# Compressing keys and values as one chain, with the two first layers side by side in TensorE's columns

## The chip, the cores and the metric

The kernel runs on one core of a Trainium2 chip. The metric is the time on the device in microseconds (us), the median of several executions. The engines are TensorE (PE; PEld is its weight load), VectorE (DVE), ScalarE (ACT) and GpSimd (POOL); SyncE (SP) issues the DMA transfers. Each engine works through its own list of instructions in order, and waits at an instruction until what it needs is there.

## The reference

One layer on 512 tokens of width 1024, in fp32. A norm and one projection (`w_in`) feed two mixers side by side: an attention (NSA) over compressed, selected and windowed keys, and a recurrence over the tokens (RWKV7). Their outputs go through `w_out`, and a feed-forward part (1024 to 4096 to 1024) follows. The change touches the compression: of 512 tokens of keys, and the same of values, 31 overlapping blocks of 32 tokens are formed in each of two heads, and each block of 32 x 64 numbers goes through two layers:

```python
def compress_blocks(kv, pos, w1, w2):
    idx = np.arange(n_cmp)[:, None] * CMP_STRIDE + np.arange(CMP_BLOCK)[None, :]
    blocks = kv[:, idx] + pos[None, None, :, None, :]
    flat = blocks.transpose(0, 1, 3, 2, 4).reshape(B, n_cmp, NSA_KV_HEADS, CMP_BLOCK * HEAD_DIM)
    return jax.nn.gelu(flat @ w1) @ w2          # 2048 -> 128 -> 64

kc = rmsnorm(compress_blocks(kc, ck_pos, ck_w1, ck_w2), kc_g)
vc = compress_blocks(vc, cv_pos, cv_w1, cv_w2)
```

## The kernel before

**Order of the work.** The layer is written as generators (streams), each of which yields the cost of what it has issued and how long to wait before it goes on. `merge` (L129) keeps a clock of these costs and always takes the ready stream of the highest priority: the input projections of RWKV (`rw_in`, `rw_v`) and NSA (`nsa_in`), four token tiles of RWKV preparation (`rw_prep`), inverse (`rw_inv`), values (`rw_vals`) and scan (`rw_chain`), and the attention (`attns`). `run_more` runs the streams that appear later: `compress_both`, `keys` and `queries`. From the program so ordered a scheduler makes the list of each engine. A change in one stream's costs or tiles thus moves its neighbours.

**Buffers.** Tiles in SBUF come from named places with a few buffers each. Where all are taken, the next user waits until the oldest has been read for the last time:

```python
PLACES = {
    'wr': (2144, 2), 'wh': (2144, 3), 'wl': (2144, 3), ...
    'kt': (2048, 8), 'vh': (2048, 4), 'qq': (2048, 7), 'tb': (2048, 1), 'cs': (1024, 4),
}
```

Bytes per partition and number of buffers: `wr` holds `wraw`, the weights as they come from memory, in two buffers. In PSUM `ps`, `pi`, `pq` and `pz` have one bank each, `pa` and `pb` two.

**Projections.** The weights come in pieces (L428): a DMA into `wraw`, a rounded copy `whi` on ACT (L311), the rest `wlo` on DVE (L312), and three products per tile on PE (L332 to 334: hi with hi, lo with hi, hi with lo). The blocks of NSA are `cmp` (columns for the compression), `kv0`, `kv1` (tiles `128x268` on PE, `128x536` for the casts), `q0` and `q1` (`128x256`), four pieces each, and 24 matmuls per piece in `tok_cols` (L836).

**Compression.** `compress` runs for keys (`kind` 0) and then for values (`kind` 1). Its steps: blocks plus positions on POOL (`XP`, 31 blocks of two heads, 62 columns); the first layer `ph` on PE, 16 matmuls with 62 columns of weights and 128 moving columns; gelu on ACT and DVE (`t1`, in the profile `t`, and `gl`); a transpose `pgl`; its copy `gt`; the second layer `pc_`; its copy `cm`. For keys a norm (`cms`, `s`, `rs_yc`), the gain (`cd`), a transpose (`pkt`) and the copy `KCT` follow; for values the copies into `VCM` on POOL. `ROW` names the two halves of the 128 partitions.

**RWKV names.** `pb` (L556) starts DVE's work on a token tile: `kkn` and `mk` (L561, L562), `AR`, `ba`, `BK` (L566, L568; on POOL `k` and another `BK`) and `rkp` (L622). `pg` (L586) multiplies `AR` and `BK`. The inverse goes to and fro between PE and DVE: `pz` and `pd` (L681), `Tn` (L694, then transposed at L671), and at its end `pz<-Tn,QU` (L702). `pv` (L614) and `pbn` (L627) are products whose outputs alternate between the two halves of the partitions.

Of the kernel before, what the change touches and what calls it, by code (L numbers as in the profile page):

```python
# [12 lines left out]
AF = mybir.ActivationFunctionType  # L13
ALU = mybir.AluOpType
AX = mybir.AxisListType


T = 512
# [96 lines left out]
def layer(ctx: ExitStack, tc: tile.TileContext, A, cst, out):  # L115
    nc = tc.nc
    PSUM = bass.MemoryType.PSUM
    V, S, G, PE = nc.vector, nc.scalar, nc.gpsimd, nc.tensor

    def bc(ap, shape):  # L120
        return ap.to_broadcast(shape)
# [5 lines left out]
    done = {}  # L127
# [34 lines left out]
    def bank(tag, n):  # L162
        return lambda shape, name, dt=F32: psA.tile(shape, dt, name=name, tag=tag, bufs=n)

    ps, pi_, pq_, pz_ = bank("ps", 1), bank("pi", 1), bank("pq", 1), bank("pz", 1)
# [10 lines left out]
    def at(place, shape, name, dt=F32):  # L176
        size, n = PLACES[place]
        assert int(np.prod(shape[1:])) * 4 <= size
        return up.tile(shape, dt, name=name, tag=place, bufs=n)
# [10 lines left out]
    def small(n, name):  # L190
        return sm.tile([128, n], F32, name=name, tag=name, bufs=1 if n == 32 else 2)
# [12 lines left out]
    ident = identr.bitcast(F32)  # L204
# [13 lines left out]
    for q in FQ:  # L218
# [9 lines left out]
        else:  # L228
            h = int(q[1])
# [57 lines left out]
    def vec(key, j=0, n=1):  # L287
        return VEC[:, VO[key] + j:VO[key] + j + n]
# [10 lines left out]
    def rsqrt(v, n, key, p=128):  # L299

        y = small(n, "rs_y" + key)[0:p]
        G.tensor_tensor(y, v, bc(MH[0:p], [p, n]), op=ALU.pow)
        return y
# [219 lines left out]
    ROW = (slice(0, 64), slice(64, 128))  # L523
# [295 lines left out]
    GK = cp.tile([128, 3, 64], F32, name="GK")  # L819
    GB = cp.tile([128, 24], F32, name="GB")  # L820
    GT = cp.tile([128, NT, 24], F32, name="GT")
    KCT = cp.tile([128, 2, 32], F32, name="KCT")
    VCM = cp.tile([128, 2, 4, 64], F32, name="VCM")
# [23 lines left out]
        for i in range(NT):  # L847
            use(i, pas[i][:, 0:n])

    def compress(kind, ckv):  # L850

        w1 = [at('kt', [128, 4, 128], "cw1") for _ in range(4)]
        w1v = A[('cmp_k_w1', 'cmp_v_w1')[kind]][0].rearrange("(a p) h -> p a h", p=128)
        for a_ in range(4):
            nc.sync.dma_start(w1[a_], w1v[:, 4 * a_:4 * a_ + 4])
        w2 = at('cs', [128, 64], "cw2")
        nc.sync.dma_start(w2, A[('cmp_k_w2', 'cmp_v_w2')[kind]][0])
        XP = []
        for a in range(2):
            pos = vec('pk' if kind == 0 else 'pv', 8 * a, 8)  # L860
            xp = at('qq', [128, 8, 2, 31], "XP")
            for kv in range(2):
                x2 = ckv[kv][:, 16 * a:T]
                src = bass.AP(tensor=x2.tensor, offset=x2.offset, ap=[x2.ap[0], [2, 8], [16, 31]])
                G.tensor_tensor(xp[:, :, kv, :], src, bc(pos.unsqueeze(2), [128, 8, 31]), op=ALU.add)
            XP.append(xp)
        done['xp', kind] = 1
        yield 0.0, 4.0
        ph = pz_([62, 128], "ph")
        for a_ in range(16):  # L870
            PE.matmul(ph, XP[a_ // 8][:, a_ % 8].rearrange("p a b -> p (a b)"), w1[a_ // 4][:, a_ % 4, :],
                      start=a_ == 0, stop=a_ == 15)
        t1 = at('cs', [62, 128], "t1")
        gl = at('cs', [62, 128], "gl")
        S.activation(t1, ph, AF.Square)
        V.tensor_scalar(t1, t1, 0.044715, 1.0, op0=ALU.mult, op1=ALU.add)
        V.tensor_tensor(t1, t1, ph, op=ALU.mult)
        S.activation(t1, t1, AF.Tanh, scale=math.sqrt(2.0 / math.pi))
        V.scalar_tensor_tensor(gl, t1, 1.0, ph, op0=ALU.add, op1=ALU.mult)
        yield 3.4, 3.0  # L880
        pgl = pz_([128, 2, 31], "pgl")
        PE.transpose(pgl.rearrange("p k n -> p (k n)"), gl, ident[0:62, 0:62])
        gt = at('cs', [128, 2, 32], "gt")
        G.memset(gt[:, :, 31:32], 0.0)
        S.copy(gt[:, :, 0:31], pgl)
        yield 0.2, 1.0
        pc_ = pz_([32, 2, 64], "pc_")
        for kv in range(2):
            PE.matmul(pc_[:, kv, :], gt[:, kv, :], w2, start=True, stop=True)
        cm = at('cs', [32, 2, 64], "cm")  # L890
        S.activation(cm, pc_, AF.Copy, scale=0.5)
        yield 0.5, 5.0
        if kind == 0:
            sq = at('cs', [32, 2, 64], "cms")
            S.activation(sq, cm, AF.Square)
            s2 = small(2, "s2")
            V.tensor_reduce(s2[0:32], sq, axis=AX.X, op=ALU.add)
            V.tensor_scalar(s2[0:32], s2[0:32], 1.0 / 64, 1e-6, op0=ALU.mult, op1=ALU.add)
            r2 = rsqrt(s2[0:32], 2, 'c', p=32)
            V.tensor_tensor(cm, cm, bc(r2.unsqueeze(2), [32, 2, 64]), op=ALU.mult)  # L900
            cd = at('cs', [32, 2, 2, 64], "cd")
            for h in range(2):
                V.tensor_tensor(cd[:, :, h, :], cm, bc(GK[0:32, None, 2, :], [32, 2, 64]), op=ALU.mult)
            pkt = pz_([128, 2, 32], "pkt")
            for kv in range(2):
                PE.transpose(pkt[:, kv, :], cd[:, kv].rearrange("p a b -> p (a b)"), ident[0:32, 0:32])
            S.copy(KCT, pkt)
        else:
            G.memset(VCM, 0.0)
            for h in range(4):  # L910
                G.tensor_copy(VCM[32 * h:32 * h + 32, :, h, :], cm)
        done['cmp', kind] = 1

    def compress_both(ckv):
        for kind in range(2):
            yield from compress(kind, ckv[kind])

    def keys(b, kb):

# [55 lines left out]
    def nsa_in():  # L975
# [10 lines left out]
        yield from feat_cols(512, cmp_in)  # L986
        done['in', 'cmp'] = 1
        more.append((5, compress_both(ckv)))
        kb = [at('qq', [128, NT, 2, 64], "kb") for _ in range(2)]
        for j in range(NT):  # L990
# [276 lines left out]
    w1v = A['w_ff1'][0].rearrange("(k p) n -> p k n", p=128)  # L1267
# [165 lines left out]
```

## Time and profile before

| | |
|---|---|
| median of 3 runs | 785.31 us (785.08 to 786.59) |
| profiled execution | 783.81 us, span 781.9 us |
| mean granted clock of TensorE | 0.987 |
| busy: PE, DVE, ACT, POOL | 759.8, 511.8, 395.6, 175.2 us |
| share of the chain that ended last: PE, DVE, ACT, DMA | 84%, 7%, 4%, 3% |

The span runs from the first to the last instruction of the profiled execution. Busy time counts the instructions of an engine, not its waits. [...] The chain that ended last is followed back from the last instruction, at each step to what released it. The projections, compression and RWKV tiles up to the attention lie between about 100 and 250 us; the feed-forward part begins behind 440 us.

### The profile page before, as it was taken

How to read it: one execution, taken by the hardware profiler on the slowest of the kernel's cores; microseconds unless marked ns; L12 is line 12 of the kernel's file. 1: busy time of each engine (PE TensorE's matmuls, PEld its weight loads, DVE VectorE, ACT ScalarE, POOL GpSimd, SP SyncE). 2: the span in 40 equal slices, each digit the busy share in tenths (PEclk: the TensorE clock that was granted, in tenths of full speed). 3: DMA queues.
4: the chain of work that ended last, by engine and by line, in shares of the span. 5: the costliest groups of instructions: out<-in, count | busy, mean ns of one | idle time of the engine just before them, and what ended most of it. 6: DMA issues, size and time to landing. Idle time of an engine off the chain costs nothing.

```text
span 781.9 us, 18278 instructions
## 1 busy us (share of the span) xinstructions
PE 759.8 (97%) x7357; PEld 657.5 (84%) x7357; DVE 511.8 (65%) x1157; ACT 395.6 (51%) x928; POOL 175.2 (22%) x176
## 2 busy tenths in 40 slices
PE   7999999999989999999999899999999999999998
PEld 5888888889879877887788899998888999978886
DVE  6444385585586789898755888973334989853333
ACT  7343433345444867888544655673332456653330
POOL 5002032240332353434400152300001323100000
PEclk9999999999985999999999999999999999999999
DMA  7741331111000000120343053233323433133212
GB/s 235 206 133 42 94 84 44 44 29 31 15 16 1 29 3 2 30 57 9 114 149 95 17 146 108 69 104 110 96 92 103 118 102 106 62 122 95 95 54 108
DMA packets 67338, 62.00 MB, mean 79 GB/s; under 512 B 6013, under 2 KB 53299, under 8 KB 67254
## 3 DMA queue, kind: packets, MB, share of 16 engines
q1 hardware_dynamic: 67254, 60.83, 25.9%
q8 instruction: 58, 0.95, 0.5%
q14 instruction: 26, 0.21, 0.1%
HBM read 58.72 MB, written 2.10 MB: 78 GB/s over the span
## 4 chain that ended last, share of the span: by engine, by line
PE 84%; DVE 7%; ACT 4%; DMA 3%; issue 1%; SPq 1%; POOL 0%; DVEq 0%; ACTq 0%; POOLq 0%
PE pa L332 8%; PE pa L333 8%; PE pa L334 8%; PE po L332 7%; PE po L333 7%; PE po L334 7%; PE pw L333 5%; PE pw L334 5%; PE pw L332 5%; PE pg L586 2%; PE sc L1075 2%; DMA wraw<-in_w_out_dram 1%; PE py L757 1%; PE pT L1111 1%; PE pz L681 1%
## 5 line engine op out<-in xcount | busy, mean ns | idle before, releaser
L311 ACT CAST whi<-wraw 128x512 fp32r<-128x512 f32 (+1 forms) x128 | 78.7, 622 | 133.4 <-PE po L333 29.1
L312 DVE TENSOR_TENSOR wlo<-wraw,whi 128x512 fp32r<-128x512 f32 (+1 forms) x120 | 86.7, 725 | 86.1 <-ACT whi L311 80.9
L332 PE MATMUL po<-whi 128*128 128x512 f32 x256 | 100.7, 394 | 1.2 <-DVE cc L1361 1.2
L333 PE MATMUL po<-wlo,whi 128*128 128x512 f32 x256 | 101.0, 395 | 0.0
L334 PE MATMUL po<-whi,wlo 128*128 128x512 f32 x256 | 100.7, 393 | 0.0
L333 PE MATMUL pw<-TT,whi 128*128 128x256 f32 x224 | 63.2, 282 | 0.0
L334 PE MATMUL pw<-TT,wlo 128*128 128x256 f32 x224 | 63.0, 281 | 0.0
L332 PE MATMUL pw<-TT,whi 128*128 128x256 f32 x224 | 62.5, 279 | 0.0
L332 PEld LDWEIGHTS po<-whi 128*128 128x128 f32 x256 | 48.0, 188 | 13.0 <-ACT whi L311 1.6
L334 PEld LDWEIGHTS po<-whi,wlo 128*128 128x128 f32 x256 | 48.1, 188 | 11.4
L333 PEld LDWEIGHTS po<-wlo,whi 128*128 128x128 f32 x256 | 48.0, 188 | 11.0
L332 PE MATMUL pa<-XH,whi 128*128 128x512 f32 (+1 forms) x144 | 53.0, 372 | 1.5 <-ACT XH L350 1.5
L333 PE MATMUL pa<-XL,whi 128*128 128x512 f32 (+1 forms) x144 | 53.7, 374 | 0.0
L334 PE MATMUL pa<-XH,wlo 128*128 128x512 f32 (+1 forms) x144 | 52.9, 370 | 0.0
L1291 POOL TENSOR_TENSOR ws<-wq 128x512 f32<-128x512 f32 x14 | 21.5, 1536 | 138.3 <-DMA wq<-in_w_ff_dram 123.2
L311 ACT CAST whi<-ws 128x512 fp32r<-128x512 f32 x56 | 33.0, 617 | 34.7 <-DVE ws L1296 9.5
L312 DVE TENSOR_TENSOR wlo<-ws,whi 128x512 fp32r<-128x512 f32 x56 | 48.2, 870 | 3.1 <-ACT whi L311 3.0
L1089 POOL TENSOR_SCALAR P<-P,z 128x128 f32<-128x128 f32 (+3 forms) x32 | 36.1, 1138 | 60.8 <-DVE z L1038 28.5
L312 DVE TENSOR_TENSOR wlo<-H,whi 128x512 fp32r<-128x512 f32 x32 | 22.1, 690 | 42.1 <-PE po L333 37.4
L334 PE MATMUL pw<-NH,wlo 128*128 128x256 f32 x168 | 47.0, 280 | 0.0
L333 PE MATMUL pw<-NL,whi 128*128 128x256 f32 x168 | 46.8, 279 | 0.0
L332 PE MATMUL pw<-NH,whi 128*128 128x256 f32 x168 | 46.8, 279 | 0.0
(317 smaller groups left out, 2007.9 us busy)
## 6 DMA issues: line engine op xcount, KB each, us to landing
wraw<-in_w_ff_dram SPq DMA_DIRECT2D x72, 256.0 KB
wq<-in_w_ff_dram SPq DMA_DIRECT2D x56, 256.0 KB
wraw<-in_w_in_dram SPq DMA_DIRECT2D x40, 256.0 KB
wraw<-in_w_in_dram SPq DMA_DIRECT2D x8, 268.0 KB
x<-in_x_dram SPq DMA_DIRECT2D x8, 256.0 KB
y<-in_x_dram SPq DMA_DIRECT2D x8, 256.0 KB
wraw<-in_w_out_dram SPq DMA_DIRECT2D x8, 256.0 KB
wraw<-in_w_out_dram SPq DMA_DIRECT2D x16, 128.0 KB
```

What stands on the lines that cost most here:

```text
L311: S.copy(hi, raw)
L312: eng.tensor_tensor(lo, raw, hi.bitcast(F32), op=ALU.subtract)
L332: PE.matmul(o_, l[0], r[0], start=first, stop=False)
L333: PE.matmul(o_, l[0], r[1], start=False, stop=False)
L334: PE.matmul(o_, l[1], r[0], start=False, stop=last)
L586: PE.matmul(pg[:, f], BK[ROW[e], 2 * f + c].rearrange("p a b -> p (a b)"), AR[c][ROW[e], f].rearrange("p a b -> p (a b)"), start=True, sto ...
L681: PE.matmul(o_[rows, b_, :], l[rows, b_, :], r[rows, b_, :], start=True, stop=True)
L757: PE.matmul(py[ROW[a], r, f, :], YL[e][c][:, f, a, :], uv, start=not q and f == 0 and e == 0, stop=True, skip_group_check=True)
L1075: PE.matmul(sc[:, h - h0, :], Qt[:, h, :], KT[br, g, hl].rearrange("p i t -> p (i t)")[:, 0:w], start=hl == 0, stop=hl == 1)
L1089: (G if (h, br) in SCG else V).tensor_scalar(P_[:, h, 0:w], P_[:, h, 0:w], z[:, h:h + 1], None, op0=ALU.mult)
L1111: PE.transpose(pt[:, h, :], P[br][:, h, j * 128:(j + 1) * 128], ident)
L1291: G.tensor_tensor(s3, q[0][0], q[1][0], op=ALU.subtract)
```

## The change

Both kinds go through one chain. The first layers use 64 columns of the array each (31 blocks of two heads padded to 32), kind 0 in the lower half of the output's partitions, kind 1 in the upper, and their matmuls alternate. Gelu, the transpose and the copy `gt` work on 128 rows or columns at once; the second layer still has four small matmuls. The copy `cm` of both kinds is one tile, and its place is `wr` in place of `cs`. Keys' norm and `KCT` come next, and the `VCM` copies last.

```diff
-    def compress(kind, ckv):
-        w2 = at('cs', [128, 64], "cw2")
...
-            xp = at('qq', [128, 8, 2, 31], "XP")
...
-        ph = pz_([62, 128], "ph")
-        for a_ in range(16):
-            PE.matmul(ph, XP[a_ // 8][:, a_ % 8].rearrange("p a b -> p (a b)"), w1[a_ // 4][:, a_ % 4, :],
-                      start=a_ == 0, stop=a_ == 15)
-        t1 = at('cs', [62, 128], "t1")
-        gl = at('cs', [62, 128], "gl")
...
-        cm = at('cs', [32, 2, 64], "cm")
-        S.activation(cm, pc_, AF.Copy, scale=0.5)
-        yield 0.5, 5.0
...
+    def compress_both(ckv):
+        w1, XP = [], []
+        for kind in range(2):
+            w1.append([at('kt', [128, 4, 128], "cw1") for _ in range(4)])
...
+                xp = at('qq', [128, 8, 2, 32], "XP")
+                G.memset(xp[:, :, :, 31:32], 0.0)
...
+            done['xp', kind] = 1
+            yield 0.0, 2.0
+        yield 0.0, 2.0
+        ph = pz_([128, 128], "ph")
         for a_ in range(16):
+            for kind in range(2):
+                PE.matmul(ph[ROW[kind]], XP[kind][a_ // 8][:, a_ % 8].rearrange("p a b -> p (a b)"),
+                          w1[kind][a_ // 4][:, a_ % 4, :], start=a_ == 0, stop=a_ == 15, skip_group_check=True)
+        t1 = at('cs', [128, 128], "t1")
+        gl = at('cs', [128, 128], "gl")
...
+        pgl = pz_([128, 2, 2, 32], "pgl")
+        PE.transpose(pgl.rearrange("p a k n -> p (a k n)"), gl, ident)
+        gt = at('cs', [128, 2, 2, 32], "gt")
+        S.copy(gt, pgl)
         yield 0.2, 1.0
+        pc_ = pz_([32, 2, 2, 64], "pc_")
+        for kind in range(2):
+            for kv in range(2):
+                PE.matmul(pc_[:, kind, kv, :], gt[:, kind, kv, :], w2[:, kind], start=True, stop=True)
+        cm2 = at('wr', [32, 2, 2, 64], "cm")
+        S.activation(cm2, pc_, AF.Copy, scale=0.5)
+        yield 0.5, 5.0
+        cm = cm2[:, 0]
...
+        G.memset(VCM, 0.0)
+        for h in range(4):
+            G.tensor_copy(VCM[32 * h:32 * h + 32, :, h, :], cm2[:, 1])
```

Counted over the whole program, PE has one transpose fewer, DVE three instructions fewer, ACT four fewer and POOL two more. All other instructions are the same, in another order on every engine from `ph` to the end of the attention.

How the instructions now stand, at three places. A row names the line, the operation, the output, the inputs and the shape; in the changed kernel the lines behind the compression are three higher (L969 and L1053 become L972 and L1056).

First PE at the first layer of the compression. `cw` is the weight of the first layer; its numbers are buffers. Before, the first of the two passes, four buffers of kind 0:

```order
L334 MATMUL pa<-whi,XL 128x268
L871 MATMUL ph<-cw_3091,XP 62x128 x4
L871 MATMUL ph<-cw_3092,XP 62x128 x3
L586 MATMUL pg<-AR,BK 128x128 x4
L871 MATMUL ph<-cw_3092,XP 62x128
L871 MATMUL ph<-cw_3093,XP 62x128 x4
L871 MATMUL ph<-cw_3094,XP 62x128 x4
L332 MATMUL pa<-whi,XH 128x268
```

In the changed kernel, 3093 and 3094 are of kind 0, 3101 and 3102 of kind 1:

```order
L878 MATMUL ph<-cw_3101,XP 64x128
L878 MATMUL ph<-cw_3093,XP 64x128
L586 MATMUL pg<-AR,BK 128x128 x4
L878 MATMUL ph<-cw_3101,XP 64x128
L878 MATMUL ph<-cw_3093,XP 64x128
L878 MATMUL ph<-cw_3101,XP 64x128
L878 MATMUL ph<-cw_3094,XP 64x128
L878 MATMUL ph<-cw_3102,XP 64x128
```

Neighbouring matmuls now belong to different kinds, and so to different halves of the columns. The second pass, which stood some 110 rows later in the old order, is gone.

Then PE ahead of `pz<-Tn,QU` of the second token tile's inverse. `pa` are projections, `pty` and `pgt` belong to RWKV's output. Before:

```order
L681 MATMUL pd<-Z,Tn 32x32 x3
L787 MATMUL pty<-identr,YY 128x128 x4
L681 MATMUL pd<-Z,Tn 32x32 x29
L969 MATMUL pq<-identr,QD 128x128 x4
L333 MATMUL pa<-wlo,XH 128x256
L334 MATMUL pa<-whi,XL 128x256
L797 MATMUL pgt<-SG,G2P 128x128 x4
L702 MATMUL pz<-Tn,QU 32x32 x16
L1053 MATMUL pcs<-KCT,QT 128x32 x4
```

After (the rows left out are further projections `pa`):

```order
L681 MATMUL pd<-Z,Tn 32x32 x5
L787 MATMUL pty<-identr,YY 128x128 x4
L681 MATMUL pd<-Z,Tn 32x32 x27
L333 MATMUL pa<-wlo,XH 128x256
L334 MATMUL pa<-whi,XL 128x256
L332 MATMUL pa<-whi,XH 128x256
...
L333 MATMUL pa<-wlo,XH 128x256
L797 MATMUL pgt<-SG,G2P 128x128 x4
L334 MATMUL pa<-whi,XL 128x256
...
L702 MATMUL pz<-Tn,QU 32x32 x16
L334 MATMUL pa<-whi,XL 128x256
```

Two projection matmuls and `pq` stood between `pd` and `pgt`; now 25 projections stand there, and 9 more between `pgt` and `pz<-Tn,QU`, with projections behind it in place of the attention's `pcs` and `sc`.

Last DVE in the first token tile, at the last piece of block kv1 before. `KD` and `kb` belong to `keys`:

```order
L694 TENSOR_TENSOR Tn<-Tn,pd 128x256
L671 STREAM_TRANSPOSE Tn<-Tn 128x256
L934 TENSOR_TENSOR KD<-kb,KD 128x512
L312 TENSOR_TENSOR wlo<-wraw,whi 128x536
L312 TENSOR_TENSOR wlo<-wraw,whi 128x512
L934 TENSOR_TENSOR KD<-kb,KD 128x512
L694 TENSOR_TENSOR Tn<-Tn,pd 128x256
L671 STREAM_TRANSPOSE Tn<-Tn 128x256
...
L561 SCALAR_TENSOR_TENSOR kkn<-k,VEC,pb 128x128
L562 TENSOR_SCALAR mk<-ta,KAH,KAC 128x128
```

After, at the second piece of that block (the rows left out are further pairs of `kkn` and `mk`):

```order
L907 TENSOR_TENSOR cm<-cm,rs_yc 32x128
L561 SCALAR_TENSOR_TENSOR kkn<-k,VEC,pb 128x128
L562 TENSOR_SCALAR mk<-ta,KAH,KAC 128x128
...
L694 TENSOR_TENSOR Tn<-Tn,pd 128x256
L910 TENSOR_TENSOR cd<-cm,GK 32x2x64 x2
L937 TENSOR_TENSOR KD<-kb,KD 128x512
L312 TENSOR_TENSOR wlo<-wraw,whi 128x536
L575 SCALAR_TENSOR_TENSOR AR<-kkn,PP 128x4x64 x2
L671 STREAM_TRANSPOSE Tn<-Tn 128x256
```

The last `wlo` of 536 columns stood ahead of `kkn` and `mk`; now the second of four stands behind them and behind `Tn`, `cd` and `KD`, and two more come later.

## Rows read from the trace of the kernel before

**Rows 1.** Page, busy time by engine, and the granted clock in 40 slices

```profile
PE 759.8 (97%) x7357; PEld 657.5 (84%) x7357; DVE 511.8 (65%) x1157; ACT 395.6 (51%) x928; POOL 175.2 (22%) x176
...
PEclk9999999999985999999999999999999999999999
```

**Rows 2.** Windows: stretch, busy us (instructions) PE, PEld, DVE, ACT, POOL, clock, DMA

```profile
115.00:160.00 45.00, 45.00 (x707) 40.49 (x705) 26.60 (x61) 16.24 (x48) 15.81 (x23) 1.00 0.18 49
160.00:165.00 5.00, 4.64 (x41) 3.99 (x40) 4.97 (x11) 3.65 (x13) 3.13 (x5) 1.00 0.00 0
```

**Rows 3.** Chain that ended last, pieces of `ph`: start, us, what

```profile
121.38 1.67 PE ph L871 x14
...
124.13 2.11 PE ph L871 x18
...
146.49 2.33 PE ph L871 x20
...
150.71 1.45 PE ph L871 x12
```

**Rows 4.** Windows around the stretch of lower clock

```profile
225.00:230.00 5.00, 1.87 (x41) 1.64 (x41) 4.90 (x9) 2.59 (x7) 2.89 (x2) 1.00 0.16 54
230.00:250.00 20.00, 20.00 (x160) 18.50 (x161) 12.12 (x64) 10.73 (x48) 5.37 (x5) 0.51 0.01 2
250.00:255.00 5.00, 5.00 (x52) 4.61 (x51) 4.82 (x23) 2.49 (x9) 0.00 (x0) 0.93 0.00 0
```

**Rows 5.** The same chain, eight passes of `pg` at two places

```profile
181.96 1.08 PE pg L586 x8
...
244.31 2.00 PE pg L586 x8
```

**Rows 6.** Timeline of PE: start, us, what [idle before it <- releaser]

```profile
217.79 1.15 PE L556 MATMUL pb<-XA,THA 8*128 8x128 f32 x8
...
225.02 1.16 PE L797 MATMUL pgt<-SG,G2P 128*128 128x128 f32 x8 [0.20 <-ACT Y L792]
229.29 0.69 PE L702 MATMUL pz<-Tn,QU 32*32 32x32 f32 x32 [3.11 <-DVE Tn L694]
```

**Rows 7.** Timeline of DVE, from `pb` to `Tn`

```profile
218.98 0.35 DVE L561 SCALAR_TENSOR_TENSOR kkn<-k,VEC,pb 128x128 f32<-128x128 f32 x1 [1.33 <-PE pb L556]
...
223.52 3.33 DVE L568 SCALAR_TENSOR_TENSOR BK<-ba,IP 64x512 f32<-64x512 f32 x2
226.86 2.05 DVE L622 SCALAR_TENSOR_TENSOR rkp<-r,VEC,k 128x128 f32<-128x128 f32 x4
228.83 0.41 DVE L694 TENSOR_TENSOR Tn<-Tn,pd 128x256 f32<-128x256 f32 x1
```

**Rows 8.** Timeline of PE, two other waits, and the windows behind the second

```profile
165.51 0.69 PE L681 MATMUL pz<-Tn,qm 32*32 32x32 f32 x57 [0.86 <-DVE Tn L694]
...
443.50 0.38 PE L333 MATMUL pa<-NL,whi 128*128 128x256 f32 x1 [1.42 <-DVE NL L353]
...
440.00:450.00 10.00, 7.94 (x56) 7.01 (x55) 10.00 (x23) 7.16 (x19) 0.00 (x0) 1.00 0.16 46
```

**Rows 9.** Timeline of PE and chain, products in halves of 64 columns

```profile
196.05 1.09 PE L614 MATMUL pv<-identr,v 128*64 128x128 f32 x16
...
196.12 1.02 PE pv L614 x16
...
289.38 1.09 PE L1127 MATMUL pv<-pcT,VCM 128*64 128x128 f32 x8
...
162.64 1.53 PE L627 MATMUL pbn<-rkp,CT 128*64 128x128 f32 x16
```

**Rows 10.** Timelines of DVE, ACT and POOL: staging, and the copies of `VCM`

```profile
132.07 0.70 DVE L312 TENSOR_TENSOR wlo<-wraw,whi 128x536 fp32r<-128x536 f32 x1
...
135.52 0.65 ACT L311 CAST whi<-wraw 128x536 fp32r<-128x536 f32 x1
...
161.64 1.69 POOL L911 COPY VCM<-cm 32x128 f32<-32x128 f32 x4
```

**Rows 11.** Windows of the attention stretch, and one row of DVE's timeline

```profile
250.00:300.00 50.00, 48.32 (x947) 39.19 (x948) 43.68 (x141) 34.88 (x101) 20.04 (x20) 0.99 0.04 13
300.00:380.00 80.00, 78.56 (x1331) 65.11 (x1325) 71.31 (x236) 67.42 (x198) 34.99 (x30) 1.00 0.11 32
...
291.67 1.67 DVE L568 SCALAR_TENSOR_TENSOR BK<-ba,IP 64x512 f32<-64x512 f32 x2
```

More of the change, by code (lines that the diff above doesn't have):

```diff
@@ L848, in tok_cols @@
             use(i, pas[i][:, 0:n])
-    def compress(kind, ckv):
[L852 to L855, printed above, removed]
-        w2 = at('cs', [128, 64], "cw2")
[L857 to L860, printed above, removed]
-            xp = at('qq', [128, 8, 2, 31], "XP")
[L862 to L868, printed above, removed]
-        ph = pz_([62, 128], "ph")
-        for a_ in range(16):
-            PE.matmul(ph, XP[a_ // 8][:, a_ % 8].rearrange("p a b -> p (a b)"), w1[a_ // 4][:, a_ % 4, :],
-                      start=a_ == 0, stop=a_ == 15)
-        t1 = at('cs', [62, 128], "t1")
-        gl = at('cs', [62, 128], "gl")
@@ new lines, in compress_both @@
+    def compress_both(ckv):
+        w1, XP = [], []
+        for kind in range(2):
+            w1.append([at('kt', [128, 4, 128], "cw1") for _ in range(4)])
+            w1v = A[('cmp_k_w1', 'cmp_v_w1')[kind]][0].rearrange("(a p) h -> p a h", p=128)
+            for a_ in range(4):
+                nc.sync.dma_start(w1[kind][a_], w1v[:, 4 * a_:4 * a_ + 4])
+        w2 = at('cs', [128, 2, 64], "cw2")
+        for kind in range(2):
+            nc.sync.dma_start(w2[:, kind], A[('cmp_k_w2', 'cmp_v_w2')[kind]][0])
+        for kind in range(2):
+            XP.append([])
+            for a in range(2):
+                pos = vec('pk' if kind == 0 else 'pv', 8 * a, 8)
+                xp = at('qq', [128, 8, 2, 32], "XP")
+                G.memset(xp[:, :, :, 31:32], 0.0)
+                for kv in range(2):
+                    x2 = ckv[kind][kv][:, 16 * a:T]
+                    src = bass.AP(tensor=x2.tensor, offset=x2.offset, ap=[x2.ap[0], [2, 8], [16, 31]])
+                    G.tensor_tensor(xp[:, :, kv, 0:31], src, bc(pos.unsqueeze(2), [128, 8, 31]), op=ALU.add)
+                XP[kind].append(xp)
+            done['xp', kind] = 1
+            yield 0.0, 2.0
+        yield 0.0, 2.0
+        ph = pz_([128, 128], "ph")
+        for a_ in range(16):
+            for kind in range(2):
+                PE.matmul(ph[ROW[kind]], XP[kind][a_ // 8][:, a_ % 8].rearrange("p a b -> p (a b)"),
+                          w1[kind][a_ // 4][:, a_ % 4, :], start=a_ == 0, stop=a_ == 15, skip_group_check=True)
+        t1 = at('cs', [128, 128], "t1")
+        gl = at('cs', [128, 128], "gl")
@@ L880, in compress @@
         yield 3.4, 3.0
[L881 to L885, printed above, removed]
-        yield 0.2, 1.0
-        pc_ = pz_([32, 2, 64], "pc_")
-        for kv in range(2):
-            PE.matmul(pc_[:, kv, :], gt[:, kv, :], w2, start=True, stop=True)
-        cm = at('cs', [32, 2, 64], "cm")
-        S.activation(cm, pc_, AF.Copy, scale=0.5)
@@ L892, in compress @@
-        yield 0.5, 5.0
[L893 to L916, printed above, removed]
+        pgl = pz_([128, 2, 2, 32], "pgl")
+        PE.transpose(pgl.rearrange("p a k n -> p (a k n)"), gl, ident)
+        gt = at('cs', [128, 2, 2, 32], "gt")
+        S.copy(gt, pgl)
+        yield 0.2, 1.0
+        pc_ = pz_([32, 2, 2, 64], "pc_")
+        for kind in range(2):
+            for kv in range(2):
+                PE.matmul(pc_[:, kind, kv, :], gt[:, kind, kv, :], w2[:, kind], start=True, stop=True)
@@ new lines, in compress_both @@
+        cm2 = at('wr', [32, 2, 2, 64], "cm")
+        S.activation(cm2, pc_, AF.Copy, scale=0.5)
+        yield 0.5, 5.0
+        cm = cm2[:, 0]
+        sq = at('cs', [32, 2, 64], "cms")
+        S.activation(sq, cm, AF.Square)
+        s2 = small(2, "s2")
+        V.tensor_reduce(s2[0:32], sq, axis=AX.X, op=ALU.add)
+        V.tensor_scalar(s2[0:32], s2[0:32], 1.0 / 64, 1e-6, op0=ALU.mult, op1=ALU.add)
+        r2 = rsqrt(s2[0:32], 2, 'c', p=32)
+        V.tensor_tensor(cm, cm, bc(r2.unsqueeze(2), [32, 2, 64]), op=ALU.mult)
@@ new lines, in compress_both @@
+        cd = at('cs', [32, 2, 2, 64], "cd")
+        for h in range(2):
+            V.tensor_tensor(cd[:, :, h, :], cm, bc(GK[0:32, None, 2, :], [32, 2, 64]), op=ALU.mult)
+        pkt = pz_([128, 2, 32], "pkt")
+        for kv in range(2):
+            PE.transpose(pkt[:, kv, :], cd[:, kv].rearrange("p a b -> p (a b)"), ident[0:32, 0:32])
+        S.copy(KCT, pkt)
+        done['cmp', 0] = 1
+        G.memset(VCM, 0.0)
+        for h in range(4):
+            G.tensor_copy(VCM[32 * h:32 * h + 32, :, h, :], cm2[:, 1])
@@ L918, in keys @@
+        done['cmp', 1] = 1
     def keys(b, kb):
```

## The prediction

> **What bounds the kernel now.** The page comes first: TensorE (PE) is busy 97% of the span, and the granted clock falls below nine tenths in two neighbouring slices alone [rows 1]. So time comes from three places: fewer PE microseconds, fewer PE waits, a faster clock. Next the windows around the compression: PE is busy 45.00 of 45 us from 115 to 160, and 4.64 of 5 behind that [rows 2]. The two passes `ph` lie in this full stretch and stand on the chain of work with 1.67 + 2.11 + 2.33 + 1.45 = 7.56 us for 64 passes (each fp32 matmul runs as two) [rows 3]. What is saved there is saved, unless something else is late.
>
> The windows show one hole later: in 225 to 230 PE works 1.87 us of 5, and after it the granted clock is 0.51 over 20 us and 0.93 over the next 5 [rows 4]. [...] Ahead of it stands the longest wait of PE: 3.11 us before `pz<-Tn,QU`, with `Tn` (L694) as releaser [rows 6]. `pb` starts at 217.79 and takes 1.15. DVE begins with it (`kkn` at 218.98) and gets to `Tn` only at 228.83, after `ba`, `BK` and `rkp` [rows 6, 7]. Other waits are shorter; the 1.42 us before 443.50 left the clock at 1.00 [rows 8].
>
> **The change, part by part.**
>
> *The passes `ph`.* The old one uses 62 of 128 columns, one kind after the other; the new one alternates, kind 0 in columns 0 to 63, kind 1 in 64 to 127 (first pair of listings). The trace has this form: `pv` (L614) alternates halves of 64 columns with a K of 128 and 128 moving columns, and 16 passes take 1.02 us of the chain, 64 ns each with the entry and 55 from start to start [rows 9]. Where one half is used alone (`pv<-pcT,VCM`, L1127) the same 1.09 us of busy time holds eight passes in place of sixteen [rows 9]. 64 passes at 55 to 64 ns are 3.5 to 4.1 us; I take 3.85, so **-3.7**. In the worst row of such alternation, `pbn` at 162.64, 16 passes take 1.53 us [rows 9], 96 ns each, though they wait for `rkp`: -1.4 as the bound.
>
> [...]
>
> *The rest of the chain.* One transpose `pgl` fewer on PE (0.27 us for one): **-0.2**. DVE loses three instructions and ACT four of 0.2 to 0.3 us each; POOL swaps two memsets for four. That is cover, not path.
>
> *What moves.* The order differs on all engines from `ph` to the end of attention. Both kinds' results now wait in `cm`, and `cm` sits in place `wr`, one of two staging buffers for the weights of the projections. It is held from its copy out of PSUM until `cd` (DVE) and the four `VCM` copies (POOL, 1.69 us [rows 10]) have read it, so the pieces of block kv1 pass through one buffer meanwhile. A buffer costs 2.75 us from its last read (`wlo` ends 132.77) to the next cast (135.52) [rows 10], when nothing else is late. In addition the `wlo` of kv1's second piece stands behind `kkn`/`mk`, `Tn`, `cd` and `KD` (third pair of listings). Walked through with the durations above: after `pb` DVE needs 2.06 us for the eight `kkn`/`mk`, about 1.5 for `Tn`, `cd` and `KD`, and 0.7 for `wlo`, with handover 4.5; PE has 20 projection passes of 0.12 and some `pd` to run, 2.6 or so. Here PE waits 1.9 us. In the same way I find 0.95 before `pc` (for `u`, behind `s` and `kb` work), 0.45 before `paa` (`PP` and `IP` on ACT), 0.3 at the first piece and 0.5 at the next `pz`. All together **+4.1**, bounds 0 and +8 (every one twice as long). None is as long as the 3.11 after which the clock fell. The 0.86 before 165.51 of the old order [rows 8] goes: **-0.9**.
>
> *The hole at 226.* The projections now run later against RWKV. Between `pb` of tile 2 and `pz<-Tn,QU`, the old order has PE work from 218.9 to 226.2, 7.3 us. In the new one (second pair of listings) 57 projection passes stand there, 57 x 0.119 = 6.8, besides `pz`, `pd`, `pty` and `pgt`, 0.7 + 0.7 + 0.65 + 1.1: about 10.5 with the entries. DVE's chain takes 10.2 in rows 7 (218.98 to 229.17); it gets a `s` reduction and a `wlo` more (1.35), but `rkp` now stands ahead of `BK`, which then falls less on POOL's own `BK` and can take 1.67 instead of 3.33 us, as at 291.67 [rows 11]. 9.9 to 11.5 against 10.5: at most 1 us of wait is left of 3.11 + 0.20. **-3.3**, bound -2.3.
>
> *The clock.* Without the hole I expect none of the 20.3 us at half clock. PE would need half, which is the bound of 10.1 us. But DVE worked 12.1 us in 230 to 250 [rows 4]; behind it, at full clock, it is busy 43.7 of 50 and 71.3 of 80 us [rows 11], 87 to 89%. At that share the same work needs 13.7 us: 20.3 - 13.7 = **-6.6**, bounds 0 and -10.1.
>
> [...]
>
> *The end of attention.* From 300 to 380 DVE is busy 71.3 and ACT 67.4 of 80 us [rows 11], and fewer RWKV instructions are left there to fill PE: I allow **+1.5**, bounds 0 and +5.
>
> *Sum.* -3.7 - 0.2 + 4.1 - 0.9 - 3.3 - 6.6 + 1.5 = -9.1. The profiled execution took 783.81 (span 781.9 and 1.9 around it): 774.7. The median shown is 785.31, 1.5 above it: **776.2 us** for a median, -1.2%.
>
> **The rivals.**
>
> *The clock falls at another place.* In tile 3, PE has some 6.4 us of its own between `pb` and `pg` in the new order (as I count it), and DVE's way from `pb` to `BK` takes 8.6 to 9.4; the old order had more PE work in this place. A wait of 2.2 to 3.0 us is near the 3.11 that brought the slow clock. Then most of the 6.6 comes back: 782 (779 to 783.5). Against it: 1.42 us did nothing, and between 1.42 and 3.11 no row decides.
>
> *The halves don't run beside each other,* so that the change doesn't do what it says: 64 passes at the old 118 ns (7.56 by 64), +3.7, 780. `pv` speaks against it. [...]
>
> *It is given back.* If the DVE and ACT work from 250 to 380 (115 of 130 us on DVE) sets the end of attention, what PE gains earlier becomes waits: 784 to 786.5. For it: DVE's 88%. Against: PE is 98% busy in these 80 us [rows 11], so it still bounds most of them.
>
> *Slower: the staging buffer.* The third piece of kv1 can only be fetched when `cm` is free. `cd` is DVE work behind `rs_yc`, which on POOL stands behind `rs_ykk` and the `VCM` copies. If it gets free after the second piece's passes have begun, 2.75 + 0.65 + 0.7 = 4.1 us pass until the third can run, against 24 x 0.12 = 2.9 of passes and some 2 of `pv`, `pkt` and `pd`. From 2 us of delay on, the wait reaches the length of 3.11 and the clock can fall here already. That costs +2 and, with 20 us at half clock in a stretch full of PE work, +10; if the old hole stays as well, nothing is won later: 785.3 - 3.9 + 2 + 10 + 2 = about 795.
>
> **How the numbers follow.** Forecast 0.48 (768 to 779); clock falls elsewhere 0.20 (779 to 783.5); halves 0.04 (780); given back 0.12 (784 to 786.5); staging 0.16 (787 to 797). About 0.2% (1.6 us) is what a measurement of this kernel can tell from no change. Faster 0.48 + 0.20 + 0.04 = 0.72, same 0.12, slower 0.16. The low end of the range is the forecast with the bound of the clock, -3.5, a short tail, -1.5, and 3 us of fewer early waits; the high one leaves out the staging case: 768 to 787. The forecast's own range is 768 to 779.
>
> **What would show it.** Right: `ph` in 3.5 to 4.1 us on the chain, in two or three pieces; granted clock 1.00 in all windows from 225 to 255; no wait before `pz<-Tn,QU` above 1 us; new waits of PE between 130 and 155 for `u`, `ta` and `wlo`, 3 to 5 us in sum. Wrong: `ph` over 5 us; a slice of low clock anywhere between 120 and 380; a wait for `wraw` or `wlo` of 3 us at kv1; or a PE share below 0.95 in the windows from 300 to 360, where the gain would be given back.

## The result

The changed kernel is slower: a median of 796.82 us (790.19 to 799.38, 4 runs) against 785.95 (785.08 to 787.36, 4 runs) for the kernel before, a ratio of 1.0123 (95% interval 1.0087 to 1.0159). The profiled execution took 799.38 us, with a span of 797.3 and a mean granted clock, TensorE's clock as a share of its full speed, of 0.973 (before: 0.987). It is the slowest of the four, and the profiled execution of before (783.81) lies below that kernel's median; so the stages below, which come from one profiled execution of each kernel, differ by 15.4 us where the medians differ by 10.9.

Two lines of the page after, beside [rows 1]: busy time of the engines, and the granted clock in 40 slices.

```profile
PE 767.8 (96%) x7356; PEld 662.9 (83%) x7356; DVE 513.9 (64%) x1154; ACT 394.2 (49%) x924; POOL 179.9 (23%) x178
...
PEclk9999999989996979999999999999999999999999
```

PE is busy 8 us longer although it has less to do, and the clock is below nine tenths in three slices (the 9th, 13th and 15th, each 20 us long) in place of two; shorter falls don't show in slices of that length. The windows of the same stretches as in [rows 2, 4, 11] show where; the columns are those of [rows 2]:

```profile
115.00:160.00 45.00, 41.14 (x705) 36.29 (x703) 30.12 (x65) 16.77 (x46) 22.67 (x28) 0.97 0.13 34
160.00:165.00 5.00, 5.00 (x110) 4.62 (x109) 3.64 (x9) 1.58 (x3) 0.00 (x0) 0.58 0.38 103
225.00:230.00 5.00, 4.64 (x64) 4.30 (x65) 2.69 (x7) 2.02 (x5) 0.00 (x0) 1.00 0.16 52
230.00:250.00 20.00, 19.92 (x217) 17.65 (x219) 13.94 (x61) 13.10 (x50) 5.61 (x5) 0.74 0.01 2
...
250.00:300.00 50.00, 44.27 (x854) 37.52 (x847) 37.65 (x118) 26.67 (x79) 17.87 (x19) 0.83 0.04 13
300.00:380.00 80.00, 76.86 (x1288) 62.39 (x1283) 69.01 (x243) 68.79 (x209) 34.46 (x30) 1.00 0.14 45
```

From 115 to 160 PE now stands still for 3.9 of 45 us; it was full before. The hole in 225 to 230 is gone (4.64 of 5), and so is the long slow stretch behind it, but only in part: 230 to 250 has 0.74. Before, 250 to 300 had 1.7 us of idle time and a clock of 0.99; now it has 5.7 us and 0.83.

The first layer did what was forecast. The pieces of the chain that are `ph`, beside [rows 3]:

```profile
124.03 0.36 PE ph L878 x2
...
126.42 2.33 PE ph L878 x40
...
129.84 1.45 PE ph L878 x22
```

They are 0.36 + 2.33 + 1.45 = 4.14 us for the same 64 passes, 7.56 before: 65 ns a pass with the entries, 55 from start to start within a piece. What ate it up are waits of PE, here between 123 and 400 us (engine, line, who is waited for, us in total, times, longest):

```profile
PE pg L586 <- DVE BK L568: 2.5, 1, 2.5
PE pd L681 <- ACT Z L689: 2.3, 1, 2.3
PE pv L1131 <- DVE tl L1119: 1.4, 4, 0.7
PE pbn L627 <- ACT UV L618: 1.3, 2, 0.9
...
PE pl L638 <- DVE kkn L561: 1.3, 1, 1.3
```

and a clock that fell six times, after 157, 239, 256, 277, 393 and 458 us of the span, for 41 us in all, against one fall of 20.5 us before.

### The profile page after: what moved, and what is told of

Its sections match the earlier page's. It is cut to its first block, busy times and chain, and to the rows that moved or that the text cites. A ratio compares the mean times of both kernels' runs of the same rounds, so it can differ in the third digit from the quotient of the medians.

```text
span 797.3 us, 18269 instructions
## 1 busy us (share of the span) xinstructions
PE 767.8 (96%) x7356; PEld 662.9 (83%) x7356; DVE 513.9 (64%) x1154; ACT 394.2 (49%) x924; POOL 179.9 (23%) x178
## 4 chain that ended last, share of the span: by engine, by line
PE 78%; DVE 11%; ACT 6%; DMA 2%; issue 2%; SPq 0%; POOL 0%; ACTq 0%; DVEq 0%; POOLq 0%
PE pa L332 8%; PE pa L333 8%; PE pa L334 8%; PE po L332 7%; PE po L334 7%; PE po L333 7%; PE pw L333 5%; PE pw L334 5%; PE pw L332 5%; PE pg L586 2%; PE sc L1078 2%; DVE wlo L312 1%; PE pT L1114 1%; ACT whi L311 1%; DVE tl L1119 1%
## 5 line engine op out<-in xcount | busy, mean ns | idle before, releaser
L311 ACT CAST whi<-wraw 128x512 fp32r<-128x512 f32 (+1 forms) x128 | 78.7, 621 | 133.5 <-PE po L333 30.7
```

Source lines behind the costliest of these rows:

```text
L311: S.copy(hi, raw)
```

## The experiments

Twelve kernels were run. To compare them, each profiled execution is cut in three by PE's rows: stage A from the first matmul of the 21st weight piece (the 481st of 816 projection matmuls, near 121 us) to the last projection; stage B from there to the first feed-forward matmul `pw` (RWKV's later tiles, attention, output projection); the rest, which is 321 to 323 us in all of them. The start differs from run to run by up to 3 us and is left out. Idle is the stage less the busy time of PE, half clock the time at a granted clock of 0.50, worked out from the windows (in before the clock is 0.50 in each us from 231 to 250, and 1.00 from 229 to 230 and from 251 to 252). At half clock the passes `pa` of 256 columns started 0.21 us apart in the changed kernel (458.6 to 459.9), at full clock 0.12 (229.3 to 230.0); for `pg` of before see [rows 5].

| kernel | median us | A us | idle in A | half clock in A | B us | idle in B | half clock in B |
|---|---|---|---|---|---|---|---|
| before | 785.95 | 103.6 | 0.9 | 0 | 235.4 | 10.8 | 20.5 |
| changed | 796.82 | 107.2 | 4.6 | 6.8 | 245.9 | 14.8 | 34.1 |
| changed, `cm` in `cs` | 811.28 | 99.9 | 1.3 | 0 | 263.9 | 23.3 | 58.0 |
| before, `cm` in `wr` | 811.94 | 112.1 | 5.0 | 3.4 | 253.0 | 17.9 | 44.3 |
| changed, kinds in sequence | 803.85 | 102.5 | 3.3 | 0 | 249.9 | 19.4 | 30.7 |
| changed, `cs`, in sequence | 798.30 | 99.3 | 0.9 | 0 | 252.7 | 14.5 | 40.9 |
| changed, `cs`, order of before | 785.13 | 100.5 | 2.1 | 0 | 237.6 | 11.2 | 23.9 |
| changed, `wr`, order of before | 795.32 | 111.5 | 7.3 | 17.0 | 237.2 | 11.0 | 23.9 |
| before, order of changed | 802.87 | 113.2 | 6.3 | 6.8 | 243.7 | 13.6 | 30.6 |
| before, order of changed with `cs` | 814.36 | 104.4 | 2.0 | 0 | 261.8 | 22.9 | 54.6 |
| before, `Tn` earlier | 782.92 | 103.5 | 0.9 | 0 | 232.2 | 9.3 | 17.1 |
| changed, `cs`, order of before, `Tn` earlier | 781.55 | 100.5 | 2.1 | 0 | 232.9 | 9.9 | 17.1 |
| before, hole filled | 783.99 | 103.6 | 0.9 | 0 | 234.5 | 7.8 | 17.1 |
| changed, `cs`, order of before, `Tn` earlier, wait filled | 781.75 | 100.4 | 2.1 | 0 | 234.8 | 9.7 | 17.0 |

**One: where `cm` lies, and what alternating the halves brings.** Four kernels, the scheduler free to order each.

```diff
-        cm2 = at('wr', [32, 2, 2, 64], "cm")
+        cm2 = at('cs', [32, 2, 2, 64], "cm")
```

> The changed kernel with one edit: the copy cm of both kinds goes to place cs, not to the staging buffers wr. Theory A (the staging buffer held by cm delays the weights of kv1, ACT waits at their cast with Z behind it, PE gets a 2.3 us wait and 6.8 us at half clock, and the order of everything behind shifts): the waits between 140 and 158 (3.85 us) shrink to under 1.5, no half clock before 200 us, and the time is 779 to 784, at least 10 us below the changed kernel. Theory B (the loss comes later, from attention that has no RWKV work left beside it, because the one chain has fewer planned steps): the early waits go, but the time stays above 788.

Measured: 811.28 us, ratio 1.0313 (1.0292 to 1.0335), 14 us above the changed kernel. Theory A holds for stage A: it is 99.9 us, 7.3 below the changed kernel, without half clock, and 3.7 below the kernel before, which is the forecast gain. But B is 18 us longer than in the changed kernel. Theory A's time is missed for that; theory B's words are met (the early waits go, the time stays above 788), but it gave no reason for 14 us more than the changed kernel. In B stands the longest wait seen here in either stage; the waits of PE in this kernel from 123 to 487 us:

```profile
PE pg L586 <- DVE BK L568: 7.3, 1, 7.3
PE pp L736 <- ACT YY L766: 3.1, 1, 3.1
PE pty L787 <- DVE YY L782: 3.0, 2, 2.6
PE pg L586 <- DVE YR L799: 2.4, 1, 2.4
```

The 7.3 us before `pg` are those of the last token tile. On DVE work of the attention and of RWKV's output lies between `kkn` and `BK`: `kkn` is done by 276.9 (its last `pb` ends at 274.8), and `BK` only at 286.7 us.

The reverse edit in the kernel before, `cm` of each kind in `wr`:

```diff
-        cm = at('cs', [32, 2, 64], "cm")
+        cm = at('wr', [32, 2, 64], "cm")
```

> The kernel before with one edit: cm of each kind goes to place wr. First layers, gelu and transposes stay as they were before. Theory A: slower than before by 5 to 14 us (791 to 800), with a wait for Z or wlo at the pieces of kv1 and half clock there or later. Theory B: within 2 us of before, since the chain and its planned steps are those of before.

Measured: 811.94 us, ratio 1.0321 (1.03 to 1.0343), beyond what theory A had and far from theory B's 2 us. A grows by 8.5 us, and B by 17.6, though nothing in B was edited.

```diff
-        for a_ in range(16):
-            for kind in range(2):
+        for kind in range(2):
+            for a_ in range(16):
                 PE.matmul(ph[ROW[kind]], ...
```

> The changed kernel with one edit: the 16 matmuls of kind 0 are issued first, then the 16 of kind 1, so that neighbours use the same half of the columns. If halves side by side are what makes ph short: ph takes 7 to 7.6 us in place of 3.9, start to start 109 to 118 ns in place of 55. If the shorter time comes from 64 columns in place of 62 or from something else, ph stays below 4.5 us. The whole time moves with the order too: between 788 and 804 by theory A, since cm still sits in wr.

Measured: 803.85 us, ratio 1.0213 (1.0187 to 1.0239). And the same with `cm` in `cs`:

> Both edits: cm in cs and the kinds one after the other. Theory A: 783 to 788, that is the kernel with cm in cs plus 3.5 us for ph; near the kernel before, as nothing of the staging is left. Theory B: above 790.

Measured: 798.30 us, ratio 1.0147 (1.0121 to 1.0173). Between theories A (783 to 788) and B (above 790) it is B's, but the order differs again. What the two kernels tell is `ph`, 7.04 us in both by PE's rows; its pieces on the chain with `cs`:

```profile
123.40 1.02 PE ph L878 x8
...
125.50 3.26 PE ph L878 x32
...
129.85 2.76 PE ph L878 x24
```

Without alternation 64 passes take 7.04 us, 110 ns each, with it 4.14. So it is the alternation that brings most of it, 2.9 us; what else is new in the form leaves 0.5 us, from 7.56 to 7.04. What follows from these four and the changed kernel: every kernel that the scheduler ordered anew is 11 to 26 us slower than the kernel before, whatever was edited, and most of it lies in B. Theory B's reason, the number of planned steps, isn't supported by that: the kernel before with `cm` in `wr` has the old steps, and loses the most. It suggested a third theory, C: the loss is the order itself.

**Two: the order held.** A function is called behind the tracing. It ties each instruction outside the compression to its predecessor in a given order, engine by engine (no waiting, issue order alone), so that two kernels can exchange their orders; the chain's own instructions stay free. TABLE is the list of indices:

```python
traced = list(nc.cur_bb.bb.instructions)
...
tc.add_manual_dep(traced[at], prev, mybir.DependencyInfo(
    mybir.DependencyClass.NoSync, mybir.DependencyReason.DATA), reason="order")
```

> The changed kernel with cm in cs, and every instruction outside the compression held in the order that it has in the kernel before, on all engines; only the chain's own instructions stand where the scheduler puts them. Theory C (the loss is the new order of everything behind the compression, attention above all, not the chain): 780 to 783.5, that is the kernel before less the 3.7 to 4.1 us of ph and pgl; the stretch from the last projection to the first w_out matmul is 164 us as before, with one stretch of half clock of about 20 us. Rival D (the chain itself costs something later, through its tiles or its place): above 788.

Measured: 785.13 us, ratio 0.9984 (0.9973 to 0.9996). This lies between theory C's range (780 to 783.5) and rival D's (above 788): the loss of 25 us is gone, but of the gain little is left. With the order of before, A is 3.1 us shorter, and B is 237.6 against 235.4; up to 1.7 of these 2.2 us are a fall of 3.4 us at 443.8 that the profile of before hasn't. The hole is back too, in its old place in the order (timeline of PE in this kernel, beside [rows 6]):

```profile
228.15 0.69 PE L702 MATMUL pz<-Tn,QU 32*32 32x32 f32 x32 [3.13 <-DVE Tn L694]
```

> The changed kernel as it is, cm in wr, held in the same order of before. It tells what the place wr costs when the order does not give way: by theory A (the hold of a staging buffer delays kv1's weights) PE waits at kv1 for 2 to 8 us and the clock may fall there: 784 to 795. If wr costs nothing by itself: as the run with cs, 780 to 783.5.

Measured: 795.32 us, ratio 1.0115 (1.0101 to 1.0128), theory A's upper end, 10.2 us above the same kernel with `cs`, all of it in A: 111.5 against 100.5, of it 5.2 us more idle time and 17 us at half clock. The chain of waits, here after `cm` was written, shows the hold (start, us, what):

```profile
134.09 0.38 ACT cm L898
...
135.36 0.72 DVE wlo L312
136.08 0.03 DVE GA L589
136.11 2.71 DMA wraw<-in_w_in_dram
138.82 0.02 issue
138.84 0.64 ACT whi L311
139.48 0.17 ACT kb L1006
```

`wlo` ends at 136.08, and only then can the next transfer begin, since `cm` sits in the other buffer: 2.71 us of DMA, `whi`, the copies behind it on ACT, and PE waits 2.8 us before `ptb`. So the place costs 10.2 us in the order of before. Whether it costs anything in the order of the changed kernel is another question, and the next run bears on it.

> The reverse: the kernel before, with its two chains and cm in cs, its other instructions held in the order of the changed kernel. Theory C: slow, 791 to 802, with the attention stretch 8 to 15 us longer than before. Rival D: within 3 us of the kernel before.

Measured: 802.87 us, ratio 1.0213 (1.0181 to 1.0245), 0.9 above theory C's range; B is 8.3 us longer than before. A grows as well, by 9.6 us, though `cm` lies in `cs` here: 6.3 us of idle time and 6.8 at half clock, where the changed kernel with `cm` in `wr` has 4.6 and 6.8. ACT waits for the transfer that follows the late `wlo`, with `Z` behind it (timelines of DVE and ACT in this kernel):

```profile
155.44 1.23 DVE L312 TENSOR_TENSOR wlo<-wraw,whi 128x536 fp32r<-128x536 f32 x1
...
159.54 0.64 ACT L311 CAST whi<-wraw 128x536 fp32r<-128x536 f32 x1 [6.09 <-DMA wraw<-in_w_in_dram]
160.09 0.36 ACT L689 COPY Z<-pz 128x256 f32<-128x256 f32 x1
```

So in this order the waits and the half clock of A come without `cm` in a staging buffer: the new order puts `wlo` behind `kkn`, `mk`, `Tn` and `KD`, and the cast comes 2.87 us after it ends. The changed kernel's own chain with `cm` in `cs`, held in this order, wasn't run.

> The kernel before, held in the order of the changed kernel with cm in cs, which took 811 us. Theory C: 806 to 818 (811 plus the 3.9 us of ph), with a wait of 5 to 8 us before pg of the last token tile. Rival D: within 3 us of the kernel before.

Measured: 814.36 us, ratio 1.0367 (1.0337 to 1.0396), and the wait before `pg` is 7.3 us. Theory C holds in both directions: stage B follows the order, and not the kernel. Order of before: 235.4, 237.6, 237.2 us. Order of the changed kernel: 245.9 and 243.7. Order of the changed kernel with `cs`: 263.9 and 261.8. Rival D falls.

**Three: the hole and the clock.** Two DVE instructions are moved, nothing else (rows of the order on DVE, before and then):

```order
L568 SCALAR_TENSOR_TENSOR BK<-ba,IP 64x8x64 x2
L622 SCALAR_TENSOR_TENSOR rkp<-r,VEC,k 128x128 x4
L694 TENSOR_TENSOR Tn<-Tn,pd 128x256
L671 STREAM_TRANSPOSE Tn<-Tn 128x256
```

```order
L568 SCALAR_TENSOR_TENSOR BK<-ba,IP 64x8x64
L694 TENSOR_TENSOR Tn<-Tn,pd 128x256
L671 STREAM_TRANSPOSE Tn<-Tn 128x256
L568 SCALAR_TENSOR_TENSOR BK<-ba,IP 64x8x64
L622 SCALAR_TENSOR_TENSOR rkp<-r,VEC,k 128x128 x4
```

> The kernel before with two DVE instructions moved: Tn (L694) and its transpose (L671) of the second token tile's inverse go from behind rkp to between the two halves of BK. Nothing else moves. If the hole of 3.11 us before pz<-Tn,QU brings the slow clock, as the prediction had it: the hole is under 0.5 us, no half clock between 225 and 255, and the time falls by 3 us for the hole and 5 to 7 for the clock, to 776 to 779. If the clock falls because no projections are left there, hole or not: the hole goes, some 20 us of half clock stay, 782 to 784.

Measured: 782.92 us, ratio 0.9955 (0.994 to 0.997): the outcome named for the second reason. `pz` starts without a wait, a smaller one of 1.45 us takes its place three groups later, and the clock still falls. Timeline of PE and windows of this kernel:

```profile
229.03 0.69 PE L702 MATMUL pz<-Tn,QU 32*32 32x32 f32 x32
...
233.11 1.29 PE L586 MATMUL pg<-AR,BK 64*128 64x128 f32 x8 [1.45 <-DVE YR L799]
```

```profile
230.00:250.00 20.00, 18.55 (x164) 17.06 (x163) 14.72 (x71) 11.29 (x49) 6.25 (x6) 0.60 0.06 16
250.00:255.00 5.00, 5.00 (x50) 4.48 (x50) 4.39 (x21) 2.75 (x9) 0.00 (x0) 0.90 0.00 0
```

> The same move in the run that holds the changed kernel (cm in cs) in the order of before. It should win the same as the move wins on the kernel before, on top of 785.1: 775 to 778 if the hole brings the slow clock, 781 to 783 if not.

Measured: 781.55 us, ratio 0.9928 (0.9905 to 0.9951). It beats both kernels: the change with `cm` in `cs`, the order of before, and the two instructions moved. Of the 4.4 us below the 785.95 of the kernel before, some 3 come from the move alone (782.92 above). The rest, 1.4 us, would be the change's, but the runs of this kernel spread from 777.32 to 783.28.

```diff
+        if q == 2:
+            dm = pq_([128, 512], "dm")
+            for n_ in range(13):
+                PE.matmul(t4(dm), XH[0][:, 0, 0, :], xk(0)[0], start=n_ == 0, stop=n_ == 12)
         pu = pq_([128, 4, 64], "puu")
```

> The kernel before, same order, with 13 more matmuls (128x128 by 512 columns, a result that nobody reads) between pgt and pz<-Tn,QU, in the hole of 3.11 us before the stretch at half clock. If the clock falls because PE stands still there: the hole is full, pz starts at the same time, no half clock between 225 and 255, and the time falls by 5 to 7 us, to 779 to 781. If it falls because the products of the stretch itself are too small: the clock falls some us later at most, 10 to 20 us of half clock stay, and the time is within 2.5 us of before.

Measured: 783.99 us, ratio 0.9958 (0.9936 to 0.998), inconclusive by the median and telling by its runs. In the profile the hole is full, and PE has no wait above 0.2 us from 215 to 235. Even so the clock falls at 235, later than before, for 13.7 us (timeline of PE, windows):

```profile
230.65 0.69 PE L702 MATMUL pz<-Tn,QU 32*32 32x32 f32 x32 [0.18 <-DVE Tn L694]
```

```profile
230.00:235.00 5.00, 4.82 (x92) 4.12 (x90) 4.93 (x25) 2.65 (x14) 0.00 (x0) 1.00 0.18 56
235.00:250.00 15.00, 15.00 (x115) 13.77 (x116) 9.52 (x48) 8.12 (x36) 5.36 (x5) 0.55 0.01 2
250.00:255.00 5.00, 5.00 (x56) 4.39 (x55) 4.94 (x22) 4.03 (x13) 0.13 (x1) 1.00 0.00 0
```

Of 11 runs, seven had a mean clock of 0.988 or 0.989 and took 783.85 to 785.24 us, three had 0.996 or 0.997 (779.09 to 780.67), and one had 1.000 and took 778.42. So with the hole filled the fall is less certain, and it isn't the hole alone that brings it. The profiled execution is one of the seven: it has 17.1 us at half clock, these 13.7 and 3.4 more at 443, and they cost some 5.9 us (784.3, the median of the seven, less the one run of 778.4).

> The changed kernel in the order of before with Tn moved (781.6 us), and 7 such matmuls between sc and pg, in the wait of 1.45 us that took the hole's place. PE then has no wait above 0.3 us from 166 to 284. If waits alone bring the slow clock: no half clock, 774 to 777. If the small products do: the clock still falls between 230 and 250, and the time stays at 780 to 783.

Measured: 781.75 us, ratio 0.9959 (0.993 to 0.9988), with 8 runs from 777.28 to 786.52. The wait was not filled as meant: the additional matmuls themselves waited 1.47 us (for `YR`), and the clock fell. It tells nothing about waits alone.

## Why the prediction was wrong

**The passes `ph`** (-3.7): right. -3.4 (7.56 to 4.14 us), shown by the alternation undone: the alternating passes start 55 ns apart, without alternation a pass takes 110. By what mechanism the alternation saves this, no run tells.

**The early waits** (+4.1 - 0.9): right as a sum, wrong in the place. Between 140 and 158 PE waits 0.65 for `u`, 0.49 for `paa`, 2.27 for `Z` and 0.44 for `UV`, 3.85 us, and the 0.86 is gone. I had put 1.9 at kv1's second piece. It came one step later, and the chain of waits of the changed kernel shows how:

```profile
151.15 0.64 DVE wlo L312
151.78 0.02 issue
151.80 3.84 DMA wraw<-in_w_in_dram
...
155.75 0.04 ACT whi L311
155.79 0.50 issue
156.29 0.37 ACT Z L689
```

The staging buffer gets free with the end of `wlo` (151.78), the transfer takes 3.84 us, and on ACT `Z`, whose input had long been there, stands behind the `whi` that waits for it. From buffer to use this is 4.5 us to the start of `Z`, near the 4.1 that the rival "the staging buffer" had. But what holds this buffer is the `wlo` that the order puts late (`cm`, read for the last time by `cd` up to 150.55, held the other one), and the reverse run has the wait with `cm` in `cs` too. Then the clock was at half for 6.8 us, which this term left out.

**The hole at 226** (-3.3): right at its place. PE reaches `pz<-Tn,QU` at 222.08 without a wait.

**The clock** (-6.6): this step failed: "Without the hole I expect none of the 20.3 us at half clock." There were 41 us. The 20.3 come from [rows 4], an estimate: the clock taken as either 1.00 or 0.50, the 0.51 over 20 us makes 19.6 us at half clock, and the 0.93 over 5 another 0.7. The step took one hole for the whole condition, from one fall in one trace. With the hole moved away the clock fell all the same after 1.45 us of wait (17.1 us), with the hole filled it fell in most runs, and in the changed kernel it fell at 239 without a wait of PE in the 13 us ahead (window of this kernel):

```profile
226.00:239.00 13.00, 13.00 (x175) 11.68 (x173) 6.67 (x17) 7.16 (x18) 0.00 (x0) 1.00 0.01 3
```

The other half of the step, that a wait of 1.42 us "left the clock at 1.00", was one draw as well. This wait, before `pa<-NL,whi`, stands in all 14 traces with 1.41 or 1.42 us. In ten of them the clock fell there for 3.4 us, in four it didn't: before, before in the order of the changed kernel, and the two kernels with `Tn` earlier and nothing filled. Beside the last of [rows 8], the same window of the changed kernel with `cs` in the order of before:

```profile
440.00:450.00 10.00, 7.94 (x41) 7.01 (x40) 10.00 (x24) 7.27 (x20) 0.00 (x0) 0.83 0.23 66
```

The price was good: 6.6 us were taken for 20.3 at half clock, and 17.1 us cost 5.9.

**The end of attention** (+1.5) failed with it. The prediction walked through the new order as far as `pz<-Tn,QU` of the second tile and gave the 150 us behind it one allowance of at most 5. Stage B grew by 10.5: 4.0 us of idle time, and 13.6 us more at half clock, which are worth 6.8 at most (half of it, an estimate). The single wait that it did foresee there, as the rival of tile 3 (2.2 to 3.0 us), came to 2.5 (timelines of PE and DVE):

```profile
265.21 1.15 PE L556 MATMUL pb<-XA,THA 8*128 8x128 f32 x8
...
276.14 0.46 PE L586 MATMUL pg<-AR,BK 64*128 64x128 f32 x2 [2.52 <-DVE BK L568]
```

```profile
267.31 0.34 DVE L561 SCALAR_TENSOR_TENSOR kkn<-k,VEC,pb 128x128 f32<-128x128 f32 x1
...
270.74 0.08 DVE L1082 DVE_READ_ACCUMULATOR2_ANT mn<- 128x1 f32 x1
...
272.59 1.68 DVE L566 SCALAR_TENSOR_TENSOR ba<-ta,kkn 128x512 f32<-128x512 f32 x1
...
275.32 1.56 DVE L568 SCALAR_TENSOR_TENSOR BK<-ba,IP 64x512 f32<-64x512 f32 x2
```

The rival had a chance of 0.20, and its loss was counted once; that the clock falls in one place didn't keep it from falling in others.

**The staging rival** (0.16, 787 to 797, about 795) had the sign and nearly the time (796.82), and that was luck. It put 20 us at half clock at kv1 and kept the old hole; there were 6.8 us at half clock in A and 34.1 in B, and the hole was gone. In the order of before the place `wr` does cost 10.2 us. In the changed kernel no run shows a cost of its own: the 7.3 us of A against the kernel with `cs` (107.2, 99.9) compare two orders, and the kernel before, in the order of the changed one and with `cm` in `cs`, has those waits and that half clock too. What the runs show in place of the forecast is the order. In sum, from the profiled spans: 1.9 at the start, 3.6 in A (3.7 of idle time, at most 3.4 for the half clock, less 3.4 for `ph`), 10.5 in B and -0.5 in the rest make 15.4, with rounding.

The rival "it is given back" (0.12) isn't what happened, since the time grew. In the order of before, though, the 3.1 us that A wins are 0.8 in the median.

What stays open: why the scheduler's new orders are all worse in B than the old one. The runs show that they are, and in which waits; whether the old order was found by search or luck no run tells. What share the place of `cm` has in the order that the scheduler chose isn't known either. And no run separates, within B, what the waits cost from what the falls of the clock cost.

## What to carry to other kernels

Where a scheduler orders the instructions, an edit is two edits: its own work and a new order of all that follows. Hold the old order and run the edit in it, and run the old kernel in the new order; only then is the gain of the edit known (here 0.8 us in the old order and some 3 in the order of the changed kernel with `cs`, under a loss of 11 to 26). A small tile in a place whose few buffers feed transfers can cost a transfer's latency (2.71 us in the order of before), and with it what stands behind the waiting cast on its engine; a late last reader of the buffer did the same in the changed kernel (a transfer of 3.84 us, with `Z` behind the cast, 4.5 us from `wlo` to `Z`). Whether a wait brings the slow clock can't be read from one trace. A walk through a new order that stops where the edit's direct effects end misses the larger part: the longest stretch behind it needs the same walk, DVE's queue first.

## What the runs showed of the hardware

The granted clock was not the same in every execution of one program. The kernel before with the hole filled ran at a mean clock of 0.988 to 1.000 in 11 executions, and its time followed, 785.2 to 778.4 us. The changed kernel ranged from 0.973 to 0.986 and from 799.4 to 790.2 us; its slowest execution has the lowest clock and its fastest the highest. The same wait of 1.42 us came with a fall in ten of 14 traces. And in the changed kernel PE's clock fell while its rows show it busy: at 239, behind 13.00 us of work in 13 (226 to 239). In the 9 us ahead of this fall it ran `pg`, `puu`, `pq`, `py`, `pcs`, `sc` and `ptb`, products of at most 128 moving columns, without a projection among them. What brings a fall can't be told from these runs.
